# Hybrid decoder block on one core: branch gates and branch projections with tokens on the partitions, products of 512 columns, and a merge that is transposed for the output projection

## Chip, cores and metric

The kernel runs on one core of one Trainium2 chip. The metric is the device time of one execution in microseconds, before: 517.9 us, the median of three runs.

## What is computed

One decoder block on 256 tokens of width 1024, all in float32. A combined projection of x feeds two mixers (HGRN2, a gated recurrence with 8 heads, and MoBA, here plain causal attention with 8 heads) and two gates. What matters for the change is how the two branches are merged:

```python
z_a = y_a @ w_branch_a                       # (256, 1024) each
z_b = y_b @ w_branch_b
g_a, g_b = split(sigmoid(gate_logits + b_gate), 2)
mixed = (g_a * z_a + g_b * z_b) @ w_out
x = layer_norm(ALPHA * x + mixed, ln1_w, ln1_b)
h_gate, h_up = split(x @ w_ffn_in, 2)
out = layer_norm(ALPHA * x + (silu(h_gate) * h_up) @ w_ffn_down, ln2_w, ln2_b)
```

gate_logits are the last 2048 columns of the combined projection x @ w_in.

## The kernel before

**Products.** Each float32 operand is split into a high part (a cast to float32r, on ScalarE) and a low part (a subtraction, on VectorE), and a product is three matmuls per k block of 128: high x high, low x high, high x low. The weights come in tiles of 1 MB (128 partitions x 2048 elements) in the order that `plan` writes down; `stage` (lines 143 to 163) issues the load on SP's queue into one of three raw buffers, casts it to wh (line 159) and subtracts to wl (line 161), each in one of four buffers. `fetch` (line 165) hands out the next split tile and keeps three more split ahead (LOOKAHEAD = 3); `fetch(0)` splits a tile only if none is ready.

**Two forms.** `feat_pair` (line 205) makes 256 output columns per weight tile: the weights are the stationary operand, 256 tokens stream past, and the result lies with features on the partitions. `tok_chunk` (line 228) makes 512 output columns from two weight tiles: the activations are stationary, 512 weight columns stream past, once for each block of 128 tokens, and tokens lie on the partitions. hf, hq, hg, the gates gb and ga, mk, mq, za and zb use the first form, hi and mv the second. The output projection (wo) and the FFN's second product (wd) use 512 columns as well, in `rows_pass`.

**Order.** The program is traced in the order hf, hq, hi, hg, gb, ga, then mk/mq/mv, za, zb, wo, FFN. The recurrence and the attention heads are generators; `side.step()` places a step of them between products. A scheduler then orders each engine's instructions by the order of tracing and by its own simulated times, except in blocks under `manual_schedule`, where the named engines keep the order of the program. Such a block holds the start (lines 255 to 281, PE, DVE and ACT) and one the output projection with the first FFN tiles (lines 635 to 665, PE, DVE and ACT). SP and POOL queues are not named in any block.

**Start.** x transposed comes in 8 pieces of 128 KB, alternating with the first two weight tiles in pieces of 256 KB; the product hf0 runs over them piece by piece, then hf2 and hf3 use the third and fourth weight tile.

**Merge.** A gate's bias is per feature, thus per partition, and is given to the Sigmoid activation (line 439). za is multiplied into ga from PSUM (line 519). For zb, each of four pieces (lines 523 to 528) is multiplied into gb, added to ga, and ga is split into mTh and mTl, with features on the partitions as the output projection wants them.

**Output projection.** Line 636 fetches the four w_out tiles (two k blocks each, 1024 columns); three are split already, the fourth is split there. Then token block 0 runs over the four tiles (line 638), two FFN tiles are split (`prefetch(2)`), the first LayerNorm of block 0 is issued (`norm1(0)`), and token block 1 runs over the four tiles with two further `prefetch(1)` and the transposes of block 0's result (`norm1_transpose(0)`, giving x1h and x1l) ahead of its last tile. The first FFN product (`e[0][0].gate()`, tile fe) then needs x1h and x1l. PSUM is two pools of four banks: `mm` for products, `aux` for the rest; wo uses four tiles of `aux`.

Of the kernel before, what the change touches and what calls it, by code (L numbers as in the profile page):

```python
# [10 lines left out]
F32 = mybir.dt.float32  # L11
F32R = mybir.dt.float32r
U32 = mybir.dt.uint32
AF = mybir.ActivationFunctionType
# [3 lines left out]
P = 128  # L18
T = 256
NT = T // P  # L20
D = 1024
KC = D // P
# [48 lines left out]
def plan():  # L71

    tiles = []

    def add(w, k0, kn, c0, n, held=False):
        tiles.append((w, k0, kn, c0, n, held))

    def feat(w, c0, n):
        for c in range(c0, c0 + n, 256):
            add(w, 0, 8, c, 256)  # L80

    def tok(w, c0, n):
        for c in range(c0, c0 + n, 512):
            add(w, 0, 4, c, 512)
            add(w, 4, 4, c, 512)

    tok("w_in", 1024, 512)
    feat("w_in", 1536, 512)
    feat("w_in", 0, 1024)
    tok("w_in", 2048, 1024)  # L90
    feat("w_in", 3072, 1024)
    feat("w_in", 8192, 1024)
    feat("w_in", 7168, 1024)
    for c in range(2):
        feat("w_in", 5120 + c * 512, 512)
        feat("w_in", 4096 + c * 512, 512)
        tok("w_in", 6144 + c * 512, 512)
    feat("w_branch_a", 0, 1024)
    feat("w_branch_b", 0, 1024)
    for k in range(0, KC, 2):  # L100
        add("w_out", k, 2, 0, 1024)
    for j in range(0, NF, 2):
        add("w_ffn_in", 0, 8, j * P, 256, j < HOLD_IN)
        add("w_ffn_in", 0, 8, FF + j * P, 256, j < HOLD_IN)
    for k in range(0, NF, 2):
        add("w_ffn_down", k, 2, 0, 1024)
    return tiles


@with_exitstack  # L110
def hybrid_layer_kernel(ctx: ExitStack, tc, x, xT, vecs, wts, ln1_w, ln1_b, ln2_w, ln2_b, consts, out):
    nc = tc.nc
    pool = lambda name, bufs, **kw: ctx.enter_context(tc.tile_pool(name=name, bufs=bufs, **kw))
    cp = pool("cp", 1)
# [7 lines left out]
    aux = pool("aux", 4, space=PSUM)  # L122

    def slot(name, dt=F32):
        return big.tile([P, 2048], dt, tag="s8", name=name)

    def r32(ap):
        return ap.bitcast(F32)
# [6 lines left out]
    def split(dst_h, dst_l, src):  # L135
        nc.scalar.copy(dst_h, src)
        nc.vector.tensor_sub(dst_l, src, r32(dst_h))
# [27 lines left out]
    def fetch(ahead=LOOKAHEAD):  # L165
        while state["next"] < len(loads) and len(ready) < 1 + ahead:
            list(stage())
        return ready.pop(0)

    def prefetch(n):  # L170
        for _ in range(n):
            list(stage())
# [3 lines left out]
    xTh = slot("xTh", F32R).rearrange("p (k t) -> p k t", k=KC)  # L176
    xTl = slot("xTl", F32R).rearrange("p (k t) -> p k t", k=KC)
    vec = cp.tile([P, 5 * H], F32, tag="vec", name="vec")
    cst = cp.tile([P, C_END], F32, tag="cst", name="cst")
    ident = cst[:, C_ID:C_ID + P]  # L180
# [8 lines left out]
    bg = vec[:, 24:40]  # L189
# [15 lines left out]
    def feat_pair(name, ah=None, al=None):  # L205
        ah, al = (xTh, xTl) if ah is None else (ah, al)
        wh, wl = fetch()
        ps = mm.tile([P, 2, T], F32, tag="mm", name=name)
        for f in range(2):
            feat_steps(ps[:, f, :], wh, wl, f, ah, al, range(KC))  # L210
        return ps

    def feat_steps(ps, wh, wl, f, ah, al, ks, k0=0):
        wcol = slice(f * P, (f + 1) * P)
        for k in ks:
            kk = k0 + k
            nc.tensor.matmul(ps, wh[:, k, wcol], ah[:, kk, :], start=(kk == 0), stop=False)  # L217
            nc.tensor.matmul(ps, wh[:, k, wcol], al[:, kk, :], start=False, stop=False)  # L218
            nc.tensor.matmul(ps, wl[:, k, wcol], ah[:, kk, :], start=False, stop=(kk == KC - 1))  # L219
# [5 lines left out]
                for f, ps in enumerate(pss):  # L225
                    feat_steps(ps, wh, wl, f, xTh, xTl, (k,), 4 * q)

    def tok_chunk(name, evac):
        pss = [mm.tile([P, 512], F32, tag="mm", name=f"{name}_{t}") for t in range(NT)]
        for q in range(2):  # L230
            wh, wl = fetch()
            for t in range(NT):
                ts = slice(t * P, (t + 1) * P)
                for k in range(4):
                    kk = 4 * q + k
                    nc.tensor.matmul(pss[t], xTh[:, kk, ts], wh[:, k, :], start=(kk == 0), stop=False)
                    nc.tensor.matmul(pss[t], xTl[:, kk, ts], wh[:, k, :], start=False, stop=False)
                    nc.tensor.matmul(pss[t], xTh[:, kk, ts], wl[:, k, :], start=False, stop=(kk == KC - 1))
            yield
        for t in range(NT):  # L240
            evac(t, pss[t])
# [12 lines left out]
    ET = mybir.EngineType  # L254
# [27 lines left out]
    for j in range(2, 4):  # L282
        ps = feat_pair(f"hf{j}")
# [4 lines left out]
    for j in range(4):  # L288
        ps = feat_pair(f"hq{j}")
# [10 lines left out]
    yah = slot("yah", F32R).rearrange("p (h t) -> p h t", h=H)  # L300
    yal = slot("yal", F32R).rearrange("p (h t) -> p h t", h=H)
# [113 lines left out]
    side = Steps()  # L415
# [6 lines left out]
    for j in range(4):  # L422
        ps = feat_pair(f"hg{j}")
# [6 lines left out]
        side.step()  # L430


    def gates(name, b0):
        g = slot(name).rearrange("p (c t) -> p c t", c=KC)
        for j in range(4):
            ps = feat_pair(f"{name}{j}")
            for f in range(2):
                c = 2 * j + f
                nc.scalar.activation(g[:, c, :], ps[:, f, :], AF.Sigmoid, bias=bg[:, b0 + c:b0 + c + 1])
            side.step()  # L440
        return g

    gb = gates("gb", KC)
    ga = gates("ga", 0)
    side.drain()

# [4 lines left out]
    ybh = slot("ybh", F32R).rearrange("p (h t) -> p h t", h=H)  # L451
    ybl = slot("ybl", F32R).rearrange("p (h t) -> p h t", h=H)
# [59 lines left out]
        side.gens.append(moba_heads(4 * c))  # L512


    for j in range(4):
        side.step()
        ps = feat_pair(f"za{j}", yah, yal)
        cs = slice(2 * j, 2 * j + 2)
        nc.vector.tensor_mul(ga[:, cs, :], ps, ga[:, cs, :])
    side.drain()  # L520
    mTh = slot("mTh", F32R).rearrange("p (k t) -> p k t", k=KC)
    mTl = slot("mTl", F32R).rearrange("p (k t) -> p k t", k=KC)
    for j in range(4):
        ps = feat_pair(f"zb{j}", ybh, ybl)
        cs = slice(2 * j, 2 * j + 2)
        nc.vector.tensor_mul(gb[:, cs, :], ps, gb[:, cs, :])
        nc.vector.tensor_add(ga[:, cs, :], ga[:, cs, :], gb[:, cs, :])
        split(mTh[:, cs, :], mTl[:, cs, :], ga[:, cs, :])


    def bcast(name, w, b):
# [5 lines left out]
    def rows_pass(parts, lhs, t, tiles, ktot):  # L537

        ts = slice(t * P, (t + 1) * P)
        lh, ll = lhs  # L540
        for ps, n0 in parts:
            ns = slice(n0, n0 + ps.shape[1])
            for k0, wh, wl in tiles:
                for k in range(2):
                    kk = k0 + k
                    nc.tensor.matmul(ps, lh(kk)[:, ts], wh[:, k, ns], start=(kk == 0), stop=False)  # L546
                    nc.tensor.matmul(ps, lh(kk)[:, ts], wl[:, k, ns], start=False, stop=False)  # L547
                    nc.tensor.matmul(ps, ll(kk)[:, ts], wh[:, k, ns], start=False, stop=(kk == ktot - 1))  # L548
# [34 lines left out]
    ah = [slot(f"ah{i}", F32R).rearrange("p (k t) -> p k t", k=KC) for i in range(3)]  # L583
    al = [slot(f"al{i}", F32R).rearrange("p (k t) -> p k t", k=KC) for i in range(3)]

    def norm1(t):
        layer_norm("n1", t, pss[t], xr[:, t, :], wb1, x1[:, t, :])
# [45 lines left out]
    pss = [row_parts(f"wo{t}", [(aux, 512)] * 2) for t in range(NT)]  # L633
    wb2 = bcast("wb2", ln2_w, ln2_b)
    with tc.manual_schedule(engines={ET.PE, ET.DVE, ET.Activation}):
        tiles = [(2 * q,) + fetch(0) for q in range(4)]
        for q in range(4):
            rows_pass(pss[0], lhs, 0, tiles[q:q + 1], KC)
        prefetch(2)
        norm1(0)  # L640
        for q in range(4):
            if q == 3:
                norm1_transpose(0)
            rows_pass(pss[1], lhs, 1, tiles[q:q + 1], KC)
            if q < 2:
                prefetch(1)
        early = [ready.pop(0) for _ in range(4)]
        e = [[FfnEarly(t, 2 * i, *early[2 * i:2 * i + 2]) for i in range(2)] for t in range(NT)]
        e[0][0].gate()
        e[0][0].up()  # L650
        norm1(1)
        e[0][0].silu()
        e[0][1].gate()
        norm1_transpose(1)
        prefetch(2)
        e[0][1].up()
        e[0][1].silu()
        e[1][0].gate()
        e[1][0].up()
        e[0][0].transpose()  # L660
        e[0][1].transpose()
        e[1][0].silu()
        e[1][1].gate()
        e[1][1].up()
        e[1][0].transpose()
# [4 lines left out]
    for j in range(EARLY, NF, 2):  # L670
# [5 lines left out]
        i, k = divmod(j, KC)  # L676
        split(ah[i][:, k:k + 2, :], al[i][:, k:k + 2, :], sg)

    pss = [row_parts("wd0", [(aux, 512)] * 2), row_parts("wd1", [(aux, 512), (aux, 256), (mm, 256)])]
    lhs = (lambda kk: ah[kk // KC][:, kk % KC, :], lambda kk: al[kk // KC][:, kk % KC, :])  # L680
    y = slot("y").rearrange("p (t d) -> p t d", t=NT)
    tiles = []
# [8 lines left out]
    layer_norm("n2", 1, pss[1], x1[:, 1, :], wb2, y[:, 1, :], store=out[P:T, :])  # L691


_INS = ['x', 'xT', 'vecs', 'wts', 'ln1_w', 'ln1_b', 'ln2_w', 'ln2_b', 'consts']


# [27 lines left out]
```

## Time and profile before

| | us |
|---|---|
| median of 3 runs | 517.9 (517.75 to 518.09) |
| profiled execution | 517.71 |
| its span | 515.7 |
| beside the span | 2.0 |
| TensorE busy | 506.5 |
| VectorE busy | 327.2 |
| ScalarE busy | 236.1 |

Rows of the timeline have the start, the duration, engine, line, operation, output and inputs, shapes, a count where equal neighbours are merged, and in brackets the idle time before and what ended it. PE is TensorE, PEld its weight loads, DVE VectorE, ACT ScalarE, POOL GpSimd, SPq the queue that issues loads. Rows of waits read: who waited <- for whom: us in total, times, longest. Rows of groups read: line, engine, operation, tile, count | busy us, mean ns | idle before. Rows of windows read: the window, its length, then busy us and count for PE, PEld, DVE, ACT and POOL, the granted clock, the busy share of the transfer engines, GB/s. Rows of transfer queues read: packets, MB, time as a share of 16 engines over the span. Consecutive matmuls overlap in the records, so the distance of their starts, not their duration, is what one costs.

### The profile page before, as it was taken

The numbers are of one execution on the slowest core, as the hardware profiler recorded it, in microseconds if no ns is written. First come the engines' busy times: TensorE is split into PE (matmuls) and PEld (weight loads), VectorE is DVE, ScalarE is ACT, GpSimd is POOL, SyncE is SP. The second block draws the span as 40 slices with busy tenths as digits, with TensorE's granted clock in tenths as the row PEclk, the third lists the DMA queues.
The fourth block names the chain that finished last, engine by engine and source line by source line (L and its number), as shares of the span: only waits on it lengthen the run. The fifth ranks groups of instructions, "written<-read, shape, count | busy, mean of one in ns | idle before, by whom it ended". The sixth has DMA issues, their size and how long they took to land.

```text
span 515.7 us, 8629 instructions
## 1 busy us (share of the span) xinstructions
PE 506.5 (98%) x3728; PEld 484.8 (94%) x3728; DVE 327.2 (63%) x351; ACT 236.1 (46%) x267; POOL 39.9 (8%) x33
## 2 busy tenths in 40 slices
PE   8999999999999999999999999999999999999994
PEld 7999889999999998998999988999999999988884
DVE  4677799997575444775772899555445454543436
ACT  5695355444354455656442553543443344324300
POOL 0000000000110162353010001000000000000000
PEclk9999999999999999999999999999999999999998
DMA  7988453343424555444575475055554455456002
GB/s 236 354 305 323 167 186 142 128 151 131 164 83 165 168 188 216 165 163 160 179 247 232 163 275 215 5 213 198 192 209 167 165 186 210 174 168 203 39 1 81
DMA packets 15573, 91.73 MB, mean 178 GB/s; under 512 B 1840, under 2 KB 2864, under 8 KB 5552
## 3 DMA queue, kind: packets, MB, share of 16 engines
q1 hardware_dynamic: 14688, 88.04, 47.5%
q0 software_dynamic: 848, 3.15, 1.9%
q8 instruction: 29, 0.48, 0.4%
q14 instruction: 8, 0.07, 0.0%
HBM read 90.13 MB, written 1.05 MB: 177 GB/s over the span
## 4 chain that ended last, share of the span: by engine, by line
PE 98%; DMA 1%; DVE 1%; issue 0%; DVEq 0%; ACT 0%; SPq 0%
PE wd L547 4%; PE wd L546 4%; PE wd L548 4%; PE fu L217 3%; PE fg L218 3%; PE fg L217 3%; PE fg L219 3%; PE fu L218 3%; PE fu L219 3%; PE sc L343 3%; PE hf L219 2%; PE hf L217 2%; PE hf L218 2%; PE mk L219 1%; PE hq L219 1%; PE hq L218 1%
## 5 line engine op out<-in xcount | busy, mean ns | idle before, releaser
L161 DVE TENSOR_TENSOR wl<-raw,wh 128x2048 fp32r<-128x2048 f32 (+2 forms) x88 | 186.6, 2122 | 123.1 <-ACT wh L159 122.7
L159 ACT CAST wh<-raw 128x2048 fp32r<-128x2048 f32 (+2 forms) x88 | 155.8, 1772 | 186.1 <-issue 50.3
L217 PE MATMUL fg<-x1h,wh 128*128 128x256 f32 x144 | 40.8, 284 | 0.0
L217 PE MATMUL fu<-x1h,wh 128*128 128x256 f32 x144 | 40.8, 284 | 0.0
L218 PE MATMUL fg<-x1l,wh 128*128 128x256 f32 x144 | 40.8, 283 | 0.0
L219 PE MATMUL fg<-x1h,wl 128*128 128x256 f32 x144 | 40.8, 283 | 0.0
L218 PE MATMUL fu<-x1l,wh 128*128 128x256 f32 x144 | 40.7, 283 | 0.0
L219 PE MATMUL fu<-x1h,wl 128*128 128x256 f32 x144 | 40.7, 283 | 0.0
L547 PE MATMUL wd<-wl,ah 128*128 128x512 f32 (+1 forms) x110 | 38.2, 348 | 0.0
L546 PE MATMUL wd<-wh,ah 128*128 128x512 f32 (+1 forms) x110 | 38.2, 347 | 0.0
L548 PE MATMUL wd<-wh,al 128*128 128x512 f32 (+1 forms) x110 | 38.1, 347 | 0.0
L218 PEld LDWEIGHTS fg<-x1l,wh 128*128 128x128 f32 x144 | 27.6, 192 | 0.0
L219 PEld LDWEIGHTS fg<-x1h,wl 128*128 128x128 f32 x144 | 27.6, 192 | 0.0
L217 PEld LDWEIGHTS fg<-x1h,wh 128*128 128x128 f32 x144 | 27.6, 192 | 0.0
L218 PEld LDWEIGHTS fu<-x1l,wh 128*128 128x128 f32 x144 | 27.6, 192 | 0.0
L219 PEld LDWEIGHTS fu<-x1h,wl 128*128 128x128 f32 x144 | 27.6, 192 | 0.0
L217 PEld LDWEIGHTS fu<-x1h,wh 128*128 128x128 f32 x144 | 27.6, 192 | 0.0
L546 PEld LDWEIGHTS wd<-wh,ah 128*128 128x128 f32 x110 | 20.8, 189 | 2.7
L548 PEld LDWEIGHTS wd<-wh,al 128*128 128x128 f32 x110 | 20.8, 189 | 2.7
L547 PEld LDWEIGHTS wd<-wl,ah 128*128 128x128 f32 x110 | 20.8, 189 | 2.6
L217 PE MATMUL hf<-xTh,wh 128*128 128x256 f32 x64 | 19.3, 301 | 1.0 <-ACT wh L159 1.0
L219 PE MATMUL hf<-xTh,wl 128*128 128x256 f32 x64 | 19.3, 302 | 0.0
(218 smaller groups left out, 1436.5 us busy)
## 6 DMA issues: line engine op xcount, KB each, us to landing
raw<-in_wts_dram SPq DMA_DIRECT2D x78, 1024.0 KB, 4.8
raw<-in_wts_dram SPq DMA_DIRECT2D x8, 256.0 KB, 5.0
xTr<-in_xT_dram SPq DMA_DIRECT2D x8, 128.0 KB, 4.7
raw<-in_wts_dram SPq DMA_DIRECT2D x2, 512.0 KB, 7.0
xr<-in_x_dram POOLq DMA_DIRECT2D x1, 1024.0 KB, 5.4
wb<-in_ln_w_dram POOLq DMA_DIRECT2D x2, 512.0 KB, 5.7
wb<-in_ln_b_dram POOLq DMA_DIRECT2D x2, 512.0 KB, 7.4
out_dram<-y SPq DMA_DIRECT2D x4, 256.0 KB, 2.1
```

The costliest lines, as they stand in the source:

```text
L159: nc.scalar.copy(h[:, ks, :], raw[:, ks, :])
L161: eng.tensor_sub(l[:, ks, :], raw[:, ks, :], r32(h[:, ks, :]))
L217: nc.tensor.matmul(ps, wh[:, k, wcol], ah[:, kk, :], start=(kk == 0), stop=False)
L218: nc.tensor.matmul(ps, wh[:, k, wcol], al[:, kk, :], start=False, stop=False)
L219: nc.tensor.matmul(ps, wl[:, k, wcol], ah[:, kk, :], start=False, stop=(kk == KC - 1))
L343: nc.tensor.matmul(ps[:, a, :], KL[:, h, :], later(Qt, n, h, 1), start=True, stop=True)
L546: nc.tensor.matmul(ps, lh(kk)[:, ts], wh[:, k, ns], start=(kk == 0), stop=False)
L547: nc.tensor.matmul(ps, lh(kk)[:, ts], wl[:, k, ns], start=False, stop=False)
L548: nc.tensor.matmul(ps, ll(kk)[:, ts], wh[:, k, ns], start=False, stop=(kk == ktot - 1))
```

## The change

The gates and the branch projections use `tok_chunk`, which takes the activations as an argument now. Their weights are laid out for it in `plan`. The gate bias is per column now; it is loaded once into a tile of its own, the same 2048 values on all 128 partitions, by a load on POOL's queue; VectorE adds it from PSUM, and ScalarE takes the sigmoid in place. za and zb are multiplied and added with tokens on the partitions. The merged ga is transposed on TensorE in blocks of 128 x 128 (`merge_transpose`: four into one PSUM tile) and split from PSUM into mTh and mTl. The transposes of the first 512 columns stand inside zb's second chunk, those of the second 512 columns inside the output projection, ahead of the third w_out tile of token block 0; the fetch of each w_out tile moves into that loop.

```diff
@@ plan
-    feat("w_in", 8192, 1024)
-    feat("w_in", 7168, 1024)
+    tok("w_in", 8192, 1024)
+    tok("w_in", 7168, 1024)
...
-    feat("w_branch_a", 0, 1024)
-    feat("w_branch_b", 0, 1024)
+    tok("w_branch_a", 0, 1024)
+    tok("w_branch_b", 0, 1024)
@@ tok_chunk
-    def tok_chunk(name, evac):
+    def tok_chunk(name, evac, ah=None, al=None):
+        ah, al = (xTh, xTl) if ah is None else (ah, al)
...
-                    nc.tensor.matmul(pss[t], xTh[:, kk, ts], wh[:, k, :], start=(kk == 0), stop=False)
-                    nc.tensor.matmul(pss[t], xTl[:, kk, ts], wh[:, k, :], start=False, stop=False)
-                    nc.tensor.matmul(pss[t], xTh[:, kk, ts], wl[:, k, :], start=False, stop=(kk == KC - 1))
+                    nc.tensor.matmul(pss[t], ah[:, kk, ts], wh[:, k, :], start=(kk == 0), stop=False)
+                    nc.tensor.matmul(pss[t], al[:, kk, ts], wh[:, k, :], start=False, stop=False)
+                    nc.tensor.matmul(pss[t], ah[:, kk, ts], wl[:, k, :], start=False, stop=(kk == KC - 1))
@@ gates
+    bgr = cp.tile([P, 2 * D], F32, tag="bgr", name="bgr")
+    nc.gpsimd.dma_start(bgr, b_gate[0].partition_broadcast(P))
+
     def gates(name, b0):
-        g = slot(name).rearrange("p (c t) -> p c t", c=KC)
-        for j in range(4):
-            ps = feat_pair(f"{name}{j}")
-            for f in range(2):
-                c = 2 * j + f
-                nc.scalar.activation(g[:, c, :], ps[:, f, :], AF.Sigmoid, bias=bg[:, b0 + c:b0 + c + 1])
-            side.step()
+        g = slot(name).rearrange("p (t d) -> p t d", t=NT)
+        for c in range(2):
+            cs = slice(c * 512, (c + 1) * 512)
+
+            def evac(t, ps):
+                nc.vector.tensor_add(g[:, t, cs], ps, bgr[:, b0 + c * 512:b0 + (c + 1) * 512])
+                nc.scalar.activation(g[:, t, cs], g[:, t, cs], AF.Sigmoid)
+
+            for _ in tok_chunk(f"{name}{c}", evac):
+                side.step()
         return g
@@ za, zb
-    for j in range(4):
-        side.step()
-        ps = feat_pair(f"za{j}", yah, yal)
-        cs = slice(2 * j, 2 * j + 2)
-        nc.vector.tensor_mul(ga[:, cs, :], ps, ga[:, cs, :])
+    for c in range(2):
+        cs = slice(c * 512, (c + 1) * 512)
+        for _ in tok_chunk(f"za{c}", lambda t, ps: nc.vector.tensor_mul(ga[:, t, cs], ps, ga[:, t, cs]), yah, yal):
+            side.step()
...
-    for j in range(4):
-        ps = feat_pair(f"zb{j}", ybh, ybl)
-        cs = slice(2 * j, 2 * j + 2)
-        nc.vector.tensor_mul(gb[:, cs, :], ps, gb[:, cs, :])
-        nc.vector.tensor_add(ga[:, cs, :], ga[:, cs, :], gb[:, cs, :])
-        split(mTh[:, cs, :], mTl[:, cs, :], ga[:, cs, :])
+
+    def merge_transpose(c, t):
+        pt = aux.tile([P, 4, P], F32, tag="aux", name=f"mt{c}{t}")
+        for a in range(4):
+            nc.tensor.transpose(pt[:, a, :], ga[:, t, c * 512 + a * P:c * 512 + (a + 1) * P], ident)
+        ks, ts = slice(4 * c, 4 * c + 4), slice(t * P, (t + 1) * P)
+        split(mTh[:, ks, ts], mTl[:, ks, ts], pt)
+
+    def merge_chunk(c):
+        cs = slice(c * 512, (c + 1) * 512)
+
+        def merge(t, ps):
+            nc.vector.tensor_mul(gb[:, t, cs], ps, gb[:, t, cs])
+            nc.vector.tensor_add(ga[:, t, cs], ga[:, t, cs], gb[:, t, cs])
+
+        return tok_chunk(f"zb{c}", merge, ybh, ybl)
+
+    for _ in merge_chunk(0):
+        pass
+    with tc.manual_schedule(engines={ET.PE}):
+        for q, _ in enumerate(merge_chunk(1)):
+            if q == 0:
+                for t in range(NT):
+                    merge_transpose(0, t)
@@ output projection
-        tiles = [(2 * q,) + fetch(0) for q in range(4)]
+        tiles = []
         for q in range(4):
+            if q == 2:
+                for t in range(NT):
+                    merge_transpose(1, t)
+            tiles.append((2 * q,) + fetch(0))
             rows_pass(pss[0], lhs, 0, tiles[q:q + 1], KC)
@@ kernel
-    nc = _bacc.Bacc("TRN2", target_bir_lowering=False, num_devices=1)
+    nc = _bacc.Bacc("TRN2", target_bir_lowering=False, num_devices=1, dynamic_dma_scratch_size=4096)
```

The last edit makes the space that POOL's queue keeps for its descriptors smaller.

More of the change, by code (lines that the diff above doesn't have):

```diff
@@ L110, in hybrid_layer_kernel @@
 @with_exitstack
-def hybrid_layer_kernel(ctx: ExitStack, tc, x, xT, vecs, wts, ln1_w, ln1_b, ln2_w, ln2_b, consts, out):
+def hybrid_layer_kernel(ctx: ExitStack, tc, x, xT, vecs, wts, b_gate, ln1_w, ln1_b, ln2_w, ln2_b, consts, out):
     nc = tc.nc
@@ L430, in hybrid_layer_kernel @@
         side.step()
+    bgr = cp.tile([P, 2 * D], F32, tag="bgr", name="bgr")
+    nc.gpsimd.dma_start(bgr, b_gate[0].partition_broadcast(P))
     def gates(name, b0):
-        g = slot(name).rearrange("p (c t) -> p c t", c=KC)
-        for j in range(4):
-            ps = feat_pair(f"{name}{j}")
-            for f in range(2):
-                c = 2 * j + f
-                nc.scalar.activation(g[:, c, :], ps[:, f, :], AF.Sigmoid, bias=bg[:, b0 + c:b0 + c + 1])
-            side.step()
+        g = slot(name).rearrange("p (t d) -> p t d", t=NT)
[6 more added lines that the diff above has]
+                side.step()
         return g
-    gb = gates("gb", KC)
+    gb = gates("gb", D)
     ga = gates("ga", 0)
@@ L691, in hybrid_layer_kernel @@
     layer_norm("n2", 1, pss[1], x1[:, 1, :], wb2, y[:, 1, :], store=out[P:T, :])
-_INS = ['x', 'xT', 'vecs', 'wts', 'ln1_w', 'ln1_b', 'ln2_w', 'ln2_b', 'consts']
+_INS = ['x', 'xT', 'vecs', 'wts', 'b_gate', 'ln1_w', 'ln1_b', 'ln2_w', 'ln2_b', 'consts']
 def kernel(**inputs):
```

## The prediction

> **What bounds the kernel now.** I read the page's busy table first, then the waits of TensorE, then the timeline of its matmuls, and last the queues of VectorE and ScalarE where the change adds work.
>
> ```profile
> span 515.7 us, 8629 instructions
> ## 1 busy us (share of the span) xinstructions
> PE 506.5 (98%) x3728; PEld 484.8 (94%) x3728; DVE 327.2 (63%) x351; ACT 236.1 (46%) x267; POOL 39.9 (8%) x33
> ```
>
> ```profile
> PE hf L217 <- ACT wh L159: 1.0, 1, 1.0
> ```
>
> TensorE is busy for 98% of the span, and its waits hold, beside one before the warm-up, only this one of 1.0 us for the first weights. So the time is the sum of matmul pitches: whatever shortens a pitch shortens the run, and each wait of TensorE that the change opens is paid in full. A busy matmul overlaps the next one, so the pitch is read from starts:
>
> ```profile
> 31.20 0.28 PE L217 MATMUL hq<-xTh,wh 128*128 128x256 f32 x1
> ...
> 54.24 0.40 PE L236 MATMUL hi<-wh,xTh 128*128 128x512 f32 x1
> ...
> 296.40 0.40 PE L546 MATMUL wo<-wh,mTh 128*128 128x512 f32 x1
> ...
> 315.48 1.03 PE L595 MATMUL x1t<-cst,x 128*128 128x128 f32 x8
> ...
> 319.08 0.28 PE L610 MATMUL fe<-wh,x1h 128*128 128x256 f32 x1
> ```
>
> hq is a product with 1024 output columns in the 256-column form: 4 tiles x 2 halves x 8 k x 3 = 192 matmuls in 54.24 - 31.20 = 23.04 us, 0.1200 us each. The wo rows are the 512-column form: 84 matmuls in 315.48 - 296.40 = 19.08 us, 0.2271 us each.
>
> **The change part by part.** Four products (gb, ga, za, zb) go from 192 matmuls to 2 chunks x 2 tiles x 2 row blocks x 12 = 96. Each costs 96 x 0.2271 = 21.80 us instead of 23.04, so four gain 4 x 1.24 = **-4.9 us**. The weights arrive in the same 16 tiles of 1 MB, and each feeds 24 x 0.2271 = 5.45 us of TensorE instead of 5.76.
>
> [...]
>
> Sixteen transposes are added. Between 315.48 and 319.08 lie 8 transposes and 12 matmuls of 0.2271: 3.60 - 2.73 = 0.87 us for 8, **+1.75 us** for 16. They are on TensorE, thus on the path.
>
> The gates add eight VectorE additions of 128x512 from PSUM; the sigmoids become 8 larger ones in place of 16. The nearest row for the addition is the za product at 0.69 us, so 5.5 us in all.
>
> ```profile
> 109.00:141.80 32.80, 32.80 (x282) 32.80 (x282) 23.55 (x25) 14.78 (x17) 1.77 (x2) 1.00 0.41 150
> 141.80:169.30 27.50, 27.50 (x235) 27.50 (x234) 17.81 (x19) 14.01 (x18) 2.25 (x3) 1.00 0.36 121
> ```
>
> ```profile
> L519 DVE TENSOR_TENSOR ga<-za,ga 128x512 f32<-128x512 f32 x4 | 2.8, 689 | 4.5 <-PE za L219 4.5
> ```
>
> ```profile
> ACT wh L159 <- PE gb L218: 11.1, 4, 4.9
> ```
>
> VectorE (third busy figure) has 9.2 and 9.7 us free in the two gate stages, and ScalarE waits 11.1 us over gb's four tiles for TensorE to release weight buffers, so the splits are ahead. I take nothing. Queued behind an addition that waits for its product would be a weight subtraction; the cost without that cover is a rival below.
>
> The bias is now also loaded broadcast to 128 partitions, 1 MB, from POOL's queue. It has a buffer of its own and no input to wait for. Where does such a load go?
>
> ```profile
> 138.07 1.02 POOL L382 TENSOR_TENSOR ost<-ost,half 128x4 f32<-128x4 f32 x1 [137.63 <-DVE ost L381]
> ...
> 243.64 0.92 POOL L578 DMA_DIRECT2D xr<-in_x_dram  x1 [5.80 <-PE mv L238]
> ```
>
> POOL stands idle until 138 us, and xr, written in the code behind the whole branch merge, is issued at 243.64, as the last mv matmul frees its buffer and ahead of nearly all za work. POOL's loads go as early as their buffer allows, so the bias should go in the first microsecond or two, beside the first weights. There the transfer engines are full and the first weights arrive just in time:
>
> ```profile
> q1 hardware_dynamic: 14688, 88.04, 47.5%
> q0 software_dynamic: 848, 3.15, 1.9%
> ```
>
> ```profile
> 2.20:18.50 16.30, 15.28 (x99) 1.00 0.91 298
> ```
>
> ```profile
> 18.30 2.51 DVE L161 TENSOR_TENSOR wl<-raw,wh 128x1024 fp32r<-128x1024 f32 x2 [2.32 <-ACT wh L159]
> ```
>
> ```profile
> 19.72 0.28 PE L219 MATMUL hf<-xTh,wl 128*128 128x256 f32 x1
> ...
> 25.36 0.28 PE L218 MATMUL hf<-xTl,wh 128*128 128x256 f32 x1
> 25.59 0.39 PE L219 MATMUL hf<-xTh,wl 128*128 128x256 f32 x1
> ```
>
> Queue q0 moved 3.15 MB in 1.9% of 515.7 us on all 16 engines, 9.8 us, so 1.05 MB takes 3.3 us. From 2.2 to 18.5 us, where the third weight tile lands, the engines are 0.91 busy (the share before the rate in the window's row): 1.5 us is free at most. The first half of that tile's low part ends near 19.5 us and is used at 19.72: 0.2 us of slack. So the delay is 3.3 - 0.2 = 3.1 us if the free 1.5 us is not usable, and 1.6 if all of it is; zero if the load goes later or yields, and below zero it can't be, since it only adds bytes. I take the middle of the saturated case, **+2.4 us**, and keep 0 and 3.1 as ends. The next tile has no slack to give it back: its first low part holds a matmul up to 25.59, 0.23 us after the one before where the pitch is 0.12.
>
> [...]
>
> The merge changes the order in the output projection. Its ACT, DVE and PE order is written by hand. Before, the fourth w_out tile was split first; now its fetch stands behind the transposes and their two splits. Rows of before:
>
> ```profile
> 296.53 1.92 ACT L159 CAST wh<-raw 128x2048 fp32r<-128x2048 f32 x1 [3.04 <-PE zb L218]
> 298.35 1.14 ACT L136 CAST mTh<-ga 128x512 fp32r<-128x512 f32 x2
> 299.38 3.72 ACT L159 CAST wh<-raw 128x2048 fp32r<-128x2048 f32 x2
> ...
> 316.11 1.07 ACT L136 CAST x1h<-x1t 128x512 fp32r<-128x512 f32 x2 [1.20 <-PE x1t L595]
> ```
>
> ```profile
> 298.48 2.29 DVE L161 TENSOR_TENSOR wl<-raw,wh 128x2048 fp32r<-128x2048 f32 x1 [0.31 <-ACT wh L159]
> 300.69 1.28 DVE L137 TENSOR_TENSOR mTl<-ga,mTh 128x512 fp32r<-128x512 f32 x2
> 301.89 4.49 DVE L161 TENSOR_TENSOR wl<-raw,wh 128x2048 fp32r<-128x2048 f32 x2
> 306.30 0.68 DVE L554 SCALAR_TENSOR_TENSOR x<-xr,wo 128x512 f32<-128x512 f32 x1
> ...
> 312.23 2.29 DVE L161 TENSOR_TENSOR wl<-raw,wh 128x2048 fp32r<-128x2048 f32 x1
> 314.94 2.29 DVE L161 TENSOR_TENSOR wl<-raw,wh 128x2048 fp32r<-128x2048 f32 x1 [0.43 <-ACT wh L159]
> 317.15 1.28 DVE L137 TENSOR_TENSOR x1l<-x1t,x1h 128x512 fp32r<-128x512 f32 x2
> ```
>
> I count from the first wo matmul (296.40 before) as 0. After 24 matmuls, 5.45, come 8 transposes, to 6.32. ScalarE's first copy starts 0.63 later than the first transpose, as 316.11 stands to 315.48: 6.08, both copies to 7.15. VectorE's first subtraction ends near 7.3; the third matmul, due at 6.77, needs it: **wait 0.55**. This pass ends at 9.6. The fourth tile's wh runs 7.15 to 9.07, its wl 9.1 to 11.35; the pass over it reaches its second matmul at 9.83: **wait 1.5**. Behind it VectorE goes from wl to the first x1l half, 19.3 us before (298.48 to 317.8); without the mTl pair (1.2) and the gaps (0.5) 17.6, so x1l comes at 26.7. The first FFN matmul that needs it was due at 22.8; with 0.87 of transposes and 2.05 of waits 25.7: **wait 1.0**. Sum **+3.1 us**; ends 0.5, if the tile's split goes first after all, and 4.1, if VectorE comes to the transposes a microsecond late.
>
> The transposes inside zb have 5.45 us of matmuls as cover against 2 x 1.4 us of multiply and add; nothing. Head 7's output is now needed after 24 zb matmuls instead of 21 short ones; nothing.
>
> Sum: -4.9 + 1.75 + 2.4 + 3.1 = +2.35. The profiled execution took 517.7 us (2.0 beside its span), 0.2 below the median of the runs, 517.9; I make the sum against it: **520.1**.
>
> **The rivals.**
> (a) The bias load costs nothing at the start: it goes later, or waits behind the weights. Place: the first 20 us; price: the 2.4 us taken back; from a delay of the third tile below 1.2 us on, the result is no longer slower (518.9 is the bound). For it: the 9% of free transfer time; against it: the saturation above. **517.7**.
> (b) The fourth tile's split still goes first; only the 0.55 is left of 3.1. Against it: the hand-written order. **517.5**.
> (c) Both: **515.1**, faster.
> (d) The additions of the gates stand ahead of weight subtractions that TensorE needs, one chunk's pair (1.4 us) per gate: **522.9**. Against it: the 11.1 us.
> (e) The change does not do what it says: 512-column products with these operands run at twice 0.1200, no gain: **525.0**. Against it: hi, mv, wo have the form already. [...]
>
> **How the numbers follow.** Forecast 0.55 (own range 518.3 to 521.8, from the ends 1.6 to 3.1 and 2.1 to 4.1), (a) 0.15, (b) 0.11, (c) 0.05, (d) 0.12, (e) 0.02. The range 516.8 to 523.0 leaves out (c), (e) and the rims of the others. About 0.2%, 1.0 us, is what a measurement of this kernel can tell from no change. Faster: (c) and the low rims of (a) and (b), 0.11. Same: the rest of (a) and (b), and the lowest part of the forecast, 0.24. Slower: 0.65.
>
> **What would show it.** The four products' matmuls at a pitch of 0.227. A POOL transfer in the first 3 us, and TensorE waits near 19 to 26 us. In the output projection, waits on the mT splits, on the fourth tile's wl and on x1l, in that order. If no bias transfer stands at the start, or if the w_out wl precedes the mT splits, my sum is wrong by that term; if TensorE waits inside gb or ga, (d) is the case.

## The result, and where the time went

The kernel with the change takes **528.6 us** (median of four runs, 528.17 to 529.85) against 518.0 beside it (517.75 to 518.72): ratio 1.0214, 95% interval 1.0202 to 1.0227. That is 10.6 us slower; the forecast was 520.1, slower by 2.2, with 523.0 as the upper end. The profiled execution took 529.85 us, its span is 527.8.

The page and TensorE's waits, after. A row of waits reads: who waited <- for whom: us in total, times, longest.

```profile
PE 510.4 (97%) x3360; PEld 469.5 (89%) x3360; DVE 333.1 (63%) x359; ACT 235.0 (45%) x259; POOL 40.4 (8%) x34
```

```profile
PE hf L217 <- ACT wh L159: 2.4, 2, 2.0
PE ot L393 <- DVE on L385: 2.3, 1, 2.3
PE mt L533 <- DVE ga L542: 1.6, 1, 1.6
PE wo L571 <- DVE wl L161: 1.1, 1, 1.1
PE warm L265 <- DVE half L266: 1.1, 1, 1.1
PE zb L237 <- ACT ybh L136: 0.5, 1, 0.5
PE po L496 <- ACT pT L493: 0.5, 1, 0.5
PE fe L635 <- DVE x1l L137: 0.4, 1, 0.4
PE wo L570 <- ACT mTh L136: 0.2, 1, 0.2
PE zb L238 <- DVE ybl L137: 0.2, 1, 0.2
```

TensorE has 368 matmuls fewer (3360 for 3728) and is still busy 3.9 us longer. Before, one wait of 1.0 us stood beside the warm-up; now nine rows stand there, 9.2 us in all. To place them, take the first matmul of every stage. These group rows of the timeline have a duration as min/median/max in ns, and then the first and last start in us; the first fence is before (hq, wo and fe are in the prediction), the second after.

```profile
L217 PE MATMUL gb<-xTh,wh x64: 281/283/364, 109.1 to 141.5; 128*128 128x256 f32 x64
L217 PE MATMUL mk<-xTh,wh x64: 278/283/469, 169.3 to 215.7; 128*128 128x256 f32 x64
L217 PE MATMUL za<-yah,wh x64: 277/283/364, 243.2 to 271.4; 128*128 128x256 f32 x64
L217 PE MATMUL fg<-x1h,wh x144: 283/283/364, 343.5 to 441.4; 128*128 128x256 f32 x144
```

```profile
L217 PE MATMUL hq<-xTh,wh x64: 283/283/283, 33.6 to 56.2; 128*128 128x256 f32 x64
L237 PE MATMUL gb<-wh,xTh x32: 388/389/478, 111.4 to 138.0; 128*128 128x512 f32 x32
L217 PE MATMUL mk<-xTh,wh x64: 277/283/469, 173.6 to 220.0; 128*128 128x256 f32 x64
L237 PE MATMUL za<-wh,yah x32: 387/389/580, 247.4 to 272.6; 128*128 128x512 f32 x32
L570 PE MATMUL wo<-wh,mTh x32: 388/389/500, 304.7 to 329.8; 128*128 128x512 f32 x32
L634 PE MATMUL fe<-wh,x1h x64: 276/283/365, 330.5 to 355.1; 128*128 128x256 f32 x64
L217 PE MATMUL fg<-x1h,wh x144: 283/283/364, 355.6 to 453.5; 128*128 128x256 f32 x144
```

Differences of neighbouring starts give the stages; the last column is the version that the experiments led to (e9, below).

| stage, us | before | after | e9 |
|---|---|---|---|
| start to hq | 31.2 | 33.6 | 32.1 |
| hq, hi, hg | 77.9 | 77.8 | 77.9 |
| gb, ga | 60.2 | 62.2 | 57.1 |
| mk to mv | 73.9 | 73.8 | 74.7 |
| za, zb | 53.2 | 57.3 | 51.9 |
| wo | 22.7 | 25.8 | 23.6 |
| fe | 24.4 | 25.1 | 24.4 |
| fg to the end | 172.2 | 172.2 | 172.1 |

Each column is one profiled execution. That of after is the slowest of its four: it loses 12.1 us against the column of before, where the medians differ by 10.6, and some 2.4 of the 12.1 are two stretches at half clock (last section). That of e9 is the slowest of its five, with 0.9 lost at the start: its column is 1.9 us below that of before, where the medians differ by 2.9.

Four places lost time. The start lost 2.4, as forecast: the bias load is POOL's first transfer, issued at 1.26, and landed 7.3 us later. wo and fe lost 3.8, 0.87 of it transposes. The two others were forecast as gains, -2.5 for the gates and -1.6 for za and zb (-2.5 and 0.87 of transposes), and came out at +2.0 and +4.1.

```profile
1.26 0.69 POOL L435 DMA_DIRECT2D bgr<-in_b_gate_dram  x1 [0.81 <-POOLq L739]
```

**Inside the gates.** Timelines of TensorE and of VectorE, after, around gb's end, and two windows of 3.41 us there (granted clock third from last):

```profile
145.56 0.44 PE L393 MATMUL ot<-cst,on 128*128 128x128 f32 x2 [2.28 <-DVE on L385]
...
150.78 0.47 PE L237 MATMUL ga<-wh,xTh 128*128 128x512 f32 x1
```

```profile
149.57 2.48 DVE L443 TENSOR_TENSOR gb<-gb,bgr 128x512 f32<-128x512 f32 x4
```

```profile
143.45:146.86 3.41, 1.29 (x11) 1.28 (x12) 2.39 (x6) 0.47 (x1) 2.06 (x2) 1.00 0.78 295
146.86:150.27 3.41, 3.41 (x18) 3.41 (x18) 2.64 (x5) 1.76 (x3) 0.00 (x0) 0.50 0.03 12
```

gb's last matmul starts at 138.4, so the product is complete near 138.8. But all four bias additions run together at 149.57, as one block. Until then the four results hold the four banks of `mm`, so ga cannot start: its first matmul is at 150.78. TensorE has only the recurrence to do meanwhile and waits 2.28 us in it. That wait names `on`, the recurrence's tile, and hides what is missing, which is ga's work. Then 3.41 us run at a granted clock of 0.50. In e1 (below), whose granted clock is 1.00 from 139.50 to 153.00, the hold on ga shows by name:

```profile
148.00 0.50 PE L237 MATMUL ga<-wh,xTh 128*128 128x512 f32 x1 [0.65 <-DVE gb L443]
```

**Inside zb.** The timeline of TensorE, after:

```profile
291.65 0.70 PE L496 MATMUL po<-pT,mv 128*128 128x256 f32 x2 [0.46 <-ACT pT L493]
...
296.74 1.68 PE L533 MATMUL mt<-cst,ga 128*128 128x128 f32 x8 [1.61 <-DVE ga L542]
...
299.08 0.63 PE L239 MATMUL zb<-wl,ybh 128*128 128x512 f32 x1
299.50 0.63 PE L237 MATMUL zb<-wh,ybh 128*128 128x512 f32 x1
```

This po row, head 7's, starts 44.2 us behind the first za matmul (247.44); before, it started 34.2 behind (243.16 to 277.40). zb0 cannot end without it, so TensorE's order puts zb1's first 24 matmuls ahead of zb0's last six. These 24 were the cover of the transposes. They are used up, and the eight transposes stand bare behind zb0's end while VectorE does two multiplications and two additions. Behind the 1.61 us of waiting the granted clock is 0.50 from 297.04 to 300.45, and the pitch 0.42 (299.08 to 299.50) instead of 0.227.

### The profile page after: what moved, and what is told of

Read it like the earlier page. It is cut to its first block, busy times and chain, and to the rows that moved or that the text cites. A ratio compares the mean times of both kernels' runs of the same rounds, so it can differ in the third digit from the quotient of the medians.

```text
span 527.8 us, 7902 instructions
## 1 busy us (share of the span) xinstructions
PE 510.4 (97%) x3360; PEld 469.5 (89%) x3360; DVE 333.1 (63%) x359; ACT 235.0 (45%) x259; POOL 40.4 (8%) x34
```

## The experiments

The theory after the result: four separate stalls, each paid in full by a TensorE that has no slack. They are the bias load beside the first weights; the gate tile, whose additions come too late to free the banks; the late heads, which take the transposes' cover; and the hand-written order of the output projection. The rival to each is that the stall is only where the time shows, and moves when it is taken away. e1 to e4 were timed beside a before of 517.6, e5 to e8 beside 517.5; after was timed in another group, beside 518.0, so differences against its 528.6 carry some 0.5 us, and are too large by that much if the kernels of these groups all ran faster by as much as their before did.

**e1, the bias load behind the first weights.** It goes to SP's queue at its place in the program.

```diff
-    nc.gpsimd.dma_start(bgr, b_gate[0].partition_broadcast(P))
+    tc.keep_in_program_order(nc.sync.dma_start(bgr, b_gate[0].partition_broadcast(P)))
```

> The changed kernel with the bias load moved from POOL's queue to SP's, in program order ahead of the weight tiles of the gates, some 90 us into the run. My theory: the 2.4 us by which hq starts later (33.6 instead of 31.2 us) are transfer time that the bias takes from the first weights, so hq starts at 31.2 again and the time falls from 528.6 to 526.2. Rival: the late start comes from the smaller descriptor space or another layout of the program, then hq stays at 33.6 and the time at 528.6.

Measured 526.83 (525.64 to 527.48), ratio 1.0183 (1.0166 to 1.0200): -1.8. hq starts at 31.5 instead of 33.6. The start's loss is the load's place.

**e2, the gate tile claimed early.** The gate's tile comes from a pool of 12 buffers that the recurrence's tiles use as well. In the program the recurrence's `on` tile now takes a buffer ahead of the gate's first write, which moved behind the whole product, and on VectorE's queue the four additions stand behind `on` and the `ya` made from it. One element written ahead of the product claims the buffer.

```diff
         g = slot(name).rearrange("p (t d) -> p t d", t=NT)
+        nc.gpsimd.memset(g[:, 0, 0:1], 0.0)
```

> The changed kernel with one element of each gate's tile written by POOL ahead of the gate's product, so that the tile takes its buffer before the recurrence's output tile does. My theory: the gate additions of gb run at 150 us only because the tile has no buffer until then, the four PSUM banks stay full, and TensorE has nothing to do: its wait of 2.3 us and the 1.9 us at double pitch behind it go, 528.6 to 524.4. Rival: VectorE is too full with the recurrence to run the additions earlier, then the wait stays and the time is 528.6, or the waits move to the weight splits.

Measured 524.47 (524.32 to 525.07), ratio 1.0135 (1.0120 to 1.0150): -4.1. The wait `ot <- on` is gone, and gb's additions, in the group rows of VectorE, now start at 123.1, as soon as the first chunk is done:

```profile
L444 DVE TENSOR_TENSOR gb<-gb,bgr x4: 682/683/692, 123.1 to 139.2; 128x512 f32<-128x512 f32 x4
```

The claim itself waits only for the last reader of an earlier tile, kq (L323), so a buffer was there for the gate from 73 us on:

```profile
73.06 0.09 POOL L439 MEMSET gb<- 128x1 f32 x1 [71.12 <-DVE kql L323]
```

That `on` holds the buffer in the changed kernel was read from the order of the program; the row of the additions there (149.57) shows their place in VectorE's queue and no wait for a buffer. That the claim brings the time back is measured; whether it does so by the buffer alone, and not also by another order of the scheduler's, was not tested apart.

**e3, the first transposes behind all of zb.**

```diff
-            if q == 0:
+            if q == 1:
                 for t in range(NT):
                     merge_transpose(0, t)
```

> The changed kernel with the eight transposes of the first 512 columns behind zb's last matmul instead of in the middle of its second chunk. My theory: head 7 comes late, the first half of the second chunk is used up to fill the time until then, so the transposes stand right behind zb's first chunk and wait for its merge, 2.0 us, and the clock's half pitch costs 1.7 more; behind the last matmul they wait at most 0.6 (for the splits), so 528.6 falls to about 525.5 and no matmul of zb runs at double pitch. Rival: the heads alone hold zb, so that the wait only moves to zb's matmuls: 528.

Measured 528.45 (528.27 to 528.89), ratio 1.0211 (1.0196 to 1.0226): nothing. My expected gain was wrong. The wait in zb went and zb kept its pitch: za and zb take 53.1 us in the profile, for 57.3 in after and 55.8 in the runs whose zb has no half clock (last section). But the output projection takes 27.9 instead of 25.8, which takes back most of the 2.7 won against 55.8. Timelines of VectorE and of TensorE, e3:

```profile
299.92 2.29 DVE L161 TENSOR_TENSOR wl<-raw,wh 128x2048 fp32r<-128x2048 f32 x1
...
303.32 1.28 DVE L137 TENSOR_TENSOR mTl<-mt,mTh 128x512 fp32r<-128x512 f32 x2
```

```profile
304.06 0.50 PE L572 MATMUL wo<-wh,mTl 128*128 128x512 f32 x1 [1.71 <-DVE mTl L137]
```

mTl stands on VectorE behind a weight subtraction of 2.29 us and two parts of the merge (the rows left out, 1.4 us). Moving the transposes takes them from one bare place to another; what they need is matmuls behind the merge, and room on VectorE.

**e4, the w_out tiles fetched ahead of the output projection,** as before the change.

```diff
-        tiles = []
+        tiles = [(2 * q,) + fetch(0) for q in range(4)]
         for q in range(4):
...
-            tiles.append((2 * q,) + fetch(0))
```

> The changed kernel with the four fetches of w_out ahead of the loop again, as before the change. My theory: the wait of 1.1 us on the fourth tile's low part and that of 0.4 on x1l go, the one of 0.4 on the transposed halves stays: 528.6 to 527.1. Rival: VectorE makes up for the late tile, or the wait only moves to x1l: 528.6.

Measured 526.69 (526.25 to 526.99), ratio 1.0175 (1.0160 to 1.0190): -1.9. The waits `wo <- wl` and `fe <- x1l` are gone, `wo <- mTh` of 0.2 stays, and wo takes 24.4 us (303.2 to 327.6) instead of 25.8.

**e5, zb freed of the heads.** This kernel leaves the second branch out of the merge: zb reads the first branch's activations, while the heads still run. It asks whether the late heads or a slow merge leave the transposes bare.

```diff
-        return tok_chunk(f"zb{c}", merge, ybh, ybl)
+        return tok_chunk(f"zb{c}", merge, yah, yal)
```

> The zb product reads the other branch's activations (yah, yal) in place of ybh, ybl, so the second branch is left out of the sum; the attention heads still run in full. Theory (late heads): in the changed kernel head 7 comes 44.3 us behind the first za matmul, zb0 cannot end before it, zb1's first 24 matmuls are used up while zb0 waits, and the transposes then stand bare behind zb0. With zb free of the heads the waits zb<-ybh 0.46, zb<-ybl 0.17 and mt<-ga 1.61 and most of po<-pT 0.46 go, and with them the stretch at half pitch where one follows: 528.6 - 2.5 = 526.1, down to 524.5 where the half pitch was in the timed runs. Rival (the merge is late on VectorE whatever zb waits for): the wait mt<-ga of 1.6 stays, 528.

Measured 524.79 (524.05 to 525.78), ratio 1.0148 (1.0127 to 1.0169): -3.8, at the far end of the theory's span. The transposes, in TensorE's timeline of e5, follow without a wait (no bracket in the row):

```profile
292.66 1.04 PE L533 MATMUL mt<-cst,ga 128*128 128x128 f32 x8
```

za and zb take 52.0 us (247.0 to 299.0) instead of 57.3, or of 55.8 without the half clock. Head 7 is as late as in after, 45.0 us behind za's start (292.01), and nothing waits for it. The rival, a merge that is late whatever zb waits for, falls.

**e6, zb in halves:** both column chunks take heads 0 to 3 first, then both take heads 4 to 7.

```diff
-    tok("w_branch_b", 0, 1024)
+    for k in (0, 4):
+        for c in (0, 512):
+            add("w_branch_b", k, 4, c, 512)
...
+        for q, c in ((0, 0), (0, 1), (1, 0), (1, 1)):
+            wh, wl = fetch()
+            for t in range(NT):
+                if (q, c, t) == (1, 1, 1):
+                    merge_transpose(0, 0)
+                    merge_transpose(0, 1)
```

> The whole computation; zb's four weight tiles come row block by row block (both column chunks of heads 0 to 3, then both of heads 4 to 7), and the first chunk's transposes stand 12 zb matmuls before the end. Theory (late heads): head 7 is now needed only behind 96 za and 57 zb matmuls, 34.7 us, and the heads' own some 6 us on TensorE, thus about 41 us behind za's start instead of some 30, and the transposes have 12 matmuls, 2.7 us, as cover against a merge of 1.4: the mt wait goes, a wait of 0 to 3 us for ybh stays if the heads are as late as before (44.3): 525.4 to 528. Rival (the merge is late on VectorE): mt keeps a wait above 1 us and the time stays at 528.

Measured 526.0 (525.57 to 526.8), ratio 1.0167 (1.0152 to 1.0182): -2.6. The transposes' wait is gone, and one of 0.5 us for ybl stays. So the heads' lateness can be met in the real computation by asking for them later.

**e7, the three mends of e1, e2 and e4 together.**

> The three mends that were tried alone, together: the bias load behind the first weights, the gate tile claimed by a one-element write, and the w_out tiles fetched ahead of the output projection. Theory (three separate stalls, each paid in full): 528.6 - 1.8 - 4.1 - 1.9 = 520.8. Rival (the losses hide one another): 522.5 to 524.

Measured 519.99 (518.95 to 521.19), ratio 1.0049 (1.0030 to 1.0067), against 520.8 expected. The losses add up and do not hide one another.

**e8, the three mends, zb in halves, and the heads' steps ahead of each za half.**

```diff
+        side.step(2)
         for _ in tok_chunk(f"za{c}", lambda t, ps: nc.vector.tensor_mul(ga[:, t, cs], ps, ga[:, t, cs]), yah, yal):
-            side.step()
+            side.step(2)
```

> The three mends, zb in halves, and the heads' steps put ahead of each za half instead of behind it. Theory: 520.8 less the 2.5 to 4 us that zb lost = 517 to 518.3, about the time before, as the gain of the products (4.9) pays for the transposes (1.75) and a few waits that stay. Below 517 if the heads now come in time. Rival (something else than the named stalls holds the time, such as the heads' chain itself): 520 or more, with a wait for ybh above 3 us.

Measured 517.37 (516.84 to 518.31, ten runs), ratio 0.9998 (0.9988 to 1.0008): the time of before. One wait is left in zb. Timelines of VectorE and TensorE, e8:

```profile
281.51 2.29 DVE L163 TENSOR_TENSOR wl<-raw,wh 128x2048 fp32r<-128x2048 f32 x1 [2.13 <-ACT wh L161]
283.72 0.42 DVE L139 TENSOR_TENSOR ybl<-po,ybh 128x256 fp32r<-128x256 f32 x1
```

```profile
284.19 0.51 PE L554 MATMUL zb<-wh,ybl 128*128 128x512 f32 x1 [1.21 <-DVE ybl L139]
```

Head 7's low part is behind a weight subtraction of 2.29 us on VectorE, as mTl was in e3.

**e9, head 7 last and the second transposes six matmuls earlier.** In the half that first needs heads 4 to 7, both row tiles take heads 4 to 6 and then head 7; in the output projection the transposes stand between the two column halves of the second w_out tile.

```diff
+            if (q, c) == (1, 0):
+                passes = [(t, range(3)) for t in range(NT)] + [(t, (3,)) for t in range(NT)]
...
-            if q == 2:
+            rows_pass(pss[0][:1], lhs, 0, tiles[q:q + 1], KC)
+            if q == 1:
                 for t in range(NT):
                     merge_transpose(1, t)
-            rows_pass(pss[0], lhs, 0, tiles[q:q + 1], KC)
+            rows_pass(pss[0][1:], lhs, 0, tiles[q:q + 1], KC)
```

> e8 with two moves and nothing left out: in the zb half that first needs heads 4 to 7 both row tiles take heads 4, 5 and 6 first and head 7 last, so that head 7's output is needed 9 matmuls, 2.04 us, later; and the second chunk's transposes stand 18 output projection matmuls in instead of 24, so that 6 matmuls, 1.36 us, cover their first copy. Theory (the named waits are paid in full): e8's wait zb<-ybl of 1.21 and wo<-mTh of 0.24 with the small gaps behind it (0.3) go: 517.4 - 1.7 = 515.7, thus 0.3% below the kernel before. Rival (the merge, which now starts 2 us later for the first row tile, is late for the transposes): mt waits 0.5 to 1, 516.5 to 517.4.

Measured **514.68** (514.35 to 515.99, five runs) against 517.57, ratio 0.9941 (0.9928 to 0.9955): 2.9 us faster than before. All of TensorE's waits in e9, and the stage starts of the table's last column:

```profile
PE warm L267 <- DVE half L268: 1.1, 1, 1.1
PE hf L219 <- ACT wh L161: 1.0, 1, 1.0
PE hf L221 <- DVE wl L163: 0.8, 2, 0.6
```

```profile
L219 PE MATMUL hq<-xTh,wh x64: 283/283/283, 32.1 to 54.8; 128*128 128x256 f32 x64
L239 PE MATMUL gb<-wh,xTh x32: 388/389/478, 110.0 to 136.5; 128*128 128x512 f32 x32
L219 PE MATMUL mk<-xTh,wh x64: 277/283/469, 167.1 to 214.4; 128*128 128x256 f32 x64
L239 PE MATMUL za<-wh,yah x32: 387/389/397, 241.8 to 266.9; 128*128 128x512 f32 x32
L579 PE MATMUL wo<-wh,mTh x32: 389/389/476, 293.7 to 316.6; 128*128 128x512 f32 x32
L643 PE MATMUL fe<-wh,x1h x64: 278/283/365, 317.3 to 341.2; 128*128 128x256 f32 x64
L219 PE MATMUL fg<-x1h,wh x144: 283/283/364, 341.7 to 439.6; 128*128 128x256 f32 x144
```

Behind the start no wait of TensorE is left. Only then does the time show what the change itself is worth.

## Why the prediction was wrong, step by step

One price first, that of eight transposes, from TensorE's timeline of e8:

```profile
290.20 1.03 PE L537 MATMUL mt<-cst,ga 128*128 128x128 f32 x8
290.99 0.48 PE L553 MATMUL zb<-wh,ybh 128*128 128x512 f32 x1
291.31 0.40 PE L554 MATMUL zb<-wh,ybl 128*128 128x512 f32 x1
```

They take 0.79 us, and the matmul behind them 0.32 instead of 0.227: 0.88.

- **Products, -4.9, and transposes, +1.75: right.** Together -3.15. e9, which has both and no further wait behind the start, is 2.9 below before. By stage in e9, the gates gain 3.1 and mk to mv lose 0.8, as some of the recurrence's matmuls fall behind the gates' end: -2.3 against -2.5. za and zb gain 1.3 with eight transposes in them, against 2.5 - 0.87 = 1.6. Eight transposes cost 0.88 in the rows above, against 0.87 taken. The pitch of the prediction's rows held in the new products: 26 gb matmuls of after start 0.2276 us apart (117.77 to 123.46), where the sum has 0.2271.
- **Bias load, +2.4: right.** hq came 2.4 late, e1 took back 1.8. The load was issued at 1.26 and landed 7.3 us later, and the transfers beside it were slower: the first weights' pieces of 256 KB landed 6.0 us (median) after their issue, for 5.0 in before and 4.7 in e1, and the pieces of x transposed 5.9 us, for 4.7 and 4.6. The zero end, a load that goes later or yields, did not come. The 2.4 is the profile of after; in those of e2 to e6, which load the bias at the same place, hq starts at 33.9 to 34.4, thus 2.7 to 3.2 late, so the term lies nearer the 3.1 end than the middle that was taken.
- **Output projection, waits of 0.55, 1.5 and 1.0: the mechanism right, the single waits sized high.** They came in that order, on mTh and mTl (0.24 and small gaps), on the fourth tile's wl (1.10) and on x1l (0.44). With the small gaps around them wo and fe lost 3.8, the transposes among it, against 3.05 + 0.87 = 3.9 in the sum; e4 took back 1.9.
- **"I take nothing" for the gates' additions: failed, 4.1 us.** I priced VectorE's time (5.5 us, with 9 free in each stage) and ScalarE's lead. Neither was the limit. The step passed over two resources: where the additions' output lives, and what frees the banks that hold their input. The old sigmoid wrote its tile after the first of four small products; the new addition writes after a whole chunk, when the recurrence, by the order of the program, had taken the buffer. Rival (d) stood at the right place and had the wrong mechanism: it has additions too early, ahead of weight subtractions, and they came 11 us behind the product's end.
- **"The transposes inside zb have 5.45 us of matmuls as cover ... nothing" and "Head 7's output is now needed after 24 zb matmuls instead of 21 short ones; nothing": failed, 3.8 us (e5).** The cover was counted in the program's order. TensorE's order used those 24 matmuls to bridge the wait for head 7. And I asked when head 7 was needed, not when it comes: its last product moved from 34.2 to 44.2 us behind za's start. (The need was miscounted too, on the safe side: 24 matmuls is where head 4 is needed, head 7 follows nine later.) Why the heads come 10 us later stays open. Their steps are traced behind halves of 24 long matmuls now, but in e8, which traces them ahead, head 7 still comes 41.1 us behind za's start (240.14 to 281.20), and in e6, which does not, 41.6.

With the measured sizes the prediction's own sum reads -4.9 + 1.75 + 2.4 + 2.9 (wo and fe without their transposes, 3.8 - 0.87) + 4.1 + 3.8 = +10.05, against +10.6 measured. The 0.5 between them is as much as the differences carry, and that it is no more is partly luck: 2.4 and 2.9 are stages of one profiled execution, 4.1 and 3.8 differences of medians, -4.9 and 1.75 the forecast terms.

## What to carry to other kernels

When a change makes pieces larger, ask of each result not only what it costs but from when its destination buffer is claimed and until when its source banks are held: a write that moves behind a larger piece can be passed by another user of the pool, and then the next product is locked out though no engine is full (here ga, until 150.78). Cover that is counted in program order is no cover if an earlier piece waits for something late, because the covering work is spent on that wait first (here 24 matmuls, and 1.61 us of waiting stood bare behind them); so date the late input, not its need. Stalls on an engine without slack add up (e7: 519.99 measured, 520.8 from the three mends taken singly), and a gain of 3 us shows only when all of them are gone (e9: 2.9).

## What the hardware showed

**Two stretches with waits in them were followed by a half clock.** In after's gates, above, TensorE was busy 1.29 of the 3.41 us before 146.86, and for the next 3.41 us the granted clock was 0.50. The first fence here has the same in zb, after; the second has two windows of e3, where the first was a little busier and the next ran at 1.00:

```profile
293.63:297.04 3.41, 1.63 (x8) 1.00 (x8) 2.59 (x5) 1.90 (x1) 0.00 (x0) 1.00 0.64 231
297.04:300.45 3.41, 3.41 (x14) 2.77 (x12) 3.41 (x4) 1.17 (x2) 0.00 (x0) 0.50 0.25 94
```

```profile
300.32:303.73 3.41, 1.80 (x11) 1.09 (x9) 3.41 (x4) 1.07 (x2) 0.00 (x0) 1.00 0.15 26
303.73:307.14 3.41, 3.08 (x13) 2.55 (x14) 1.47 (x3) 0.00 (x0) 0.00 (x0) 1.00 0.69 281
```

Busy 38% and 48% of 3.41 us stood before a half clock; 53%, in e3, did not. Nor did 40%: in after TensorE was busy 1.38 us between 3.51 and 6.93, and the clock was 1.00 to 17.16. So this share alone does not tell them apart. Each of the two stretches of after at 0.50 lasts 3.41 us, and they start 150.18 us apart, 44 times 3.413. Behind the last matmul the clock falls to 0.50 once more, at 525.73, which is 228.69 us or 67 times 3.413 after the second start. That falls keep to steps of this length is an estimate from these three starts of one execution.

The same wait was not always followed by a half clock. e1 has the wait for `on` too, of 2.25 us, with TensorE busy 1.76 of the 3.40 us from 139.50 to 142.90, and the clock stayed at 1.00; what makes the difference is not shown. The price shows in the stages: the gates take 62.2 and 62.5 us in after and e3, whose clock was 0.50 there (147 to 149), and 61.4 and 61.5 in e1 and e4, which ran at 1.00; za and zb take 57.3 in after and 55.8 or 55.9 in e1, e2 and e4, which have the same wait in zb at a clock of 1.00. That is about 0.9 us in the gates and 1.5 in zb.
